# Eight edits to a scheduled one-core transformer layer: sums of the start on TensorE, decay factors by ScalarE, half-row modulation, the last gate folded into w_down

## The chip, the cores and the metric

One Trainium2 chip, one NeuronCore (core 0). The metric is the device time of one execution in microseconds (us). Engines are named as in the profile: PE is TensorE's matmul stream, PEld its weight loads, DVE is VectorE, ACT is ScalarE, POOL is GpSimd, SP is the engine that issues every DMA of this kernel (SPq its queue).

## The reference, cut to what matters

Batch 1, 512 positions, width 1024, one layer, float32.

```python
mod = (silu(c) @ ada_w + ada_b)[:, None, :]
sh1, sc1, g1, sh2, sc2, g2 = jnp.split(mod, 6, axis=-1)
h = x * (1.0 + sc1) + sh1
# mixer: proj = h @ w_in (1024 x 4112), split into q, k, v (8 heads x 64), z, xBC, dt (16 columns)
#   attention: block-sparse causal, ALiBi
#   xBC = silu(causal_dwconv(xBC, 4 taps)) -> xs (16 heads x 64), B, C (2 groups x 128)
#   dt = softplus(dt_raw + dt_bias); a = -exp(a_log)
#   y = ssd_scan(xs, dt, a, B, C) + xs * d_skip     (decays exp(cumsum(dt * a)))
#   y = grouped_rms_norm(y * silu(z)) * norm_w;  o = [attention, y] @ w_out
x = layer_norm(alpha * x + (1.0 + g1) * o, ln1_g, ln1_b)
h = x * (1.0 + sc2) + sh2
u = causal_dwconv(h @ w_up, 3 taps)                 # 1024 x 5632
y = (silu(u[:, :2816]) * u[:, 2816:]) @ w_down      # 2816 x 1024
out = layer_norm(alpha * x + (1.0 + g2) * y, ln2_g, ln2_b)
```

## The kernel before, in words

**The order of work.** The kernel doesn't write its instructions down in a fixed order. Each piece of work is a Python generator ("thread") that yields one engine operation, a buffer request or a `Need` of a key at a time. `Order.run` holds a modelled clock for each engine, asks every thread for its next operation, and emits the one with the earliest modelled start; ties within a small slack go to the lowest priority number given in `R.spawn(thread, priority)`. Durations come from `Order.price`. All operations are emitted in `Order.emit`, which is line 300, so nearly every row of the profile says L300 and groups are told apart by their tiles. What results is one fixed sequence for each engine; at run time each engine works through its own, and waits for the others by semaphores. A changed price, priority or thread can therefore move any later instruction.

**Matmuls.** A float32 matrix is split into a rounded high part (ACT copy, `wh`, `hh`) and the remainder (DVE subtract, `wl`, `hl`), and each product is three passes in TensorE's rounded format: high by high, low by high, high by low. A weight item of 128x1024 values is `raw` when it has landed; `w_load` requests it and `w_split` makes `wh` and `wl`.

**The start.** `start_load` issues for each of eight blocks k of 128 channels: four 256 KB pieces of the first two modulations' weights (`aw`), the block of x (`xk`) and 128 rows of the w_in columns of B, C and four x tiles (`wr`, 128x768). For each block `start_acc` multiplies `aw` by the activated conditioning vector and adds it up on DVE into two partial sums `acc[:, 0]` and `acc[:, 1]`, and adds these two; `start_h` sums over partitions with PE (`pa`), makes `mod`, then `hh`, `hk`, `hl`. `products` runs six accumulators (`first`) over the blocks. `start_dt` loads and splits the 16 dt columns (`wdr`); `consts` loads three 16-value vectors by broadcast and builds masks.

**The mixer.** Then come the remaining projection tiles (`fm`, and `tm` for v). `dt_chain` turns the dt product (`pd`) into time steps: transposed by `pdt` with the 0/1 matrix `sel`, some 20 small DVE operations (`dd`), cumulative sums by PE (`pcs`), copied (`csT`) and written to a scratch array in DRAM (`drcs`) by four DMAs. `ssd_decay(ft)`, for each of eight pairs of heads, reads from there twice: `er` (64 partitions x 3 x 128, twice), then one ACT exponential of 128x384; and `csb`, the whole 4 KB row on all 128 partitions, masked by POOL (`affine_select`), eight ACT exponentials, two DVE multiplies by the scores `sc`, and then the stationary operand of PE's `py`. `ssd_state` makes `xe`, `pst`, `st`, `pyo`. Attention, gate, norm, out_proj (`po` from `os`), and the first layer norm follow; meanwhile `ada_mid` sums up three more modulations, and `x_rows` reads x again.

**The end.** The up projection (`up`, convolution `u`, gated product `mid`), then w_down (`dn`) in two column halves, the second in column pieces so that the last layer norm (`ln2`) can start; there `y = dn * g2p` and `XN = XN + y` on DVE, statistics `st`, `mv`, normalisation and the output DMAs.

## Time and profile before

| | us |
|---|---|
| three timed runs | 726.88, 727.51, 728.98 (median 727.51) |
| the profiled execution, own time | 729.33 |
| its span on the page | 727.6 |
| PE busy in the span | 711.1 (98%) |
| PEld, DVE, ACT, POOL busy | 582.4, 528.1, 314.3, 58.7 |
| moved by DMA | 98.95 MB, mean 136 GB/s |

The page divides the span into 40 slices; in nearly all PE is busy for nine tenths or more. Whatever the time can lose must come from the few places where PE is idle or slow, or from fewer PE passes. "Idle before, releaser" in a row is how long an engine sat idle before that instruction and what ended it. Times at the left of a timeline row are us from the start of the span, then the us that the row covers.

### The profile page before, as it was taken

To read this page: it belongs to the slowest core of one execution; us is meant where nothing else is said; L and a number is where in the kernel's file an instruction comes from. 1 tells how busy PE (TensorE), PEld (TensorE's weight loads), DVE (VectorE), ACT (ScalarE), POOL (GpSimd) and SP (SyncE) were. 2 spreads that over 40 slices of the span, in tenths; PEclk is the share of its full clock that TensorE was granted. 3 is DMA by queue.
4 is the path that set the end of the run, shared out by engine and by line. 5 is a ranking of instruction groups with operands and counts; after the bars stand their busy time and mean duration, and the time that the engine had idled before them with its cause. 6 is when DMAs were issued, how large, how long until landed. Compare 5 with 4: busy or idle time off the path is not lost.

```text
span 727.6 us, 9568 instructions
## 1 busy us (share of the span) xinstructions
PE 711.1 (98%) x3603; PEld 582.4 (80%) x3603; DVE 528.1 (73%) x935; ACT 314.3 (43%) x524; POOL 58.7 (8%) x68
## 2 busy tenths in 40 slices
PE   8999989999999999999999999999999999999995
PEld 8776867788887888788998888888888888888885
DVE  5988899999998998597865886565665664227247
ACT  2447475564665643233753443434444452212100
POOL 0010101110000011001000000000000009300022
PEclk9999999999999999999999999999999999999999
DMA  9995677426235845243623553323333254322202
GB/s 260 308 255 169 143 215 205 125 74 198 88 96 170 280 156 177 62 133 90 174 87 116 174 155 102 91 86 95 105 90 89 69 165 160 97 87 88 86 30 86
DMA packets 115831, 98.95 MB, mean 136 GB/s; under 512 B 5325, under 2 KB 97865, under 8 KB 115785
## 3 DMA queue, kind: packets, MB, share of 16 engines
q1 hardware_dynamic: 115785, 98.34, 46.0%
q8 instruction: 28, 0.46, 0.3%
q14 instruction: 18, 0.15, 0.1%
HBM read 96.20 MB, written 2.13 MB: 135 GB/s over the span
## 4 chain that ended last, share of the span: by engine, by line
PE 57%; DVE 1%; issue 0%; DVEq 0%
PE up L300 34%; PE dn L300 17%; PE po L300 6%; PE pt L300 0%; DVE XN L300 0%; PE pad L300 0%; DVE st L300 0%; DVE y L300 0%; DVE mv L300 0%; DVEq L1602 0%
## 5 line engine op out<-in xcount | busy, mean ns | idle before, releaser
L300 DVE TENSOR_TENSOR wl<-raw,wh 128x1024 fp32r<-128x1024 f32 x102 | 127.5, 1252 | 88.1 <-ACT wh L300 77.0
L300 ACT ACTIVATE wh<-raw 128x1024 fp32r<-128x1024 f32 x102 | 106.9, 1051 | 87.5 <-PE dn L300 54.5
L300 PE MATMUL up<-h2h,wh 128*128 128x512 f32 (+1 forms) x384 | 144.4, 376 | 0.0
L300 PE MATMUL up<-h2h,wl 128*128 128x512 f32 (+1 forms) x384 | 144.3, 376 | 0.0
L300 PE MATMUL up<-h2l,wh 128*128 128x512 f32 (+1 forms) x384 | 144.0, 375 | 0.0
L300 PE MATMUL dn<-wh,mid 128*128 128x512 f32 (+1 forms) x356 | 102.7, 372 | 0.0
L300 DVE SCALAR_TENSOR_TENSOR u<-up,fprm,u 128x511 f32<-128x511 f32 x88 | 65.8, 749 | 34.9 <-ACT u L300 33.3
L300 PEld LDWEIGHTS up<-h2h,wl 128*128 128x128 f32 x384 | 72.2, 188 | 14.2
L300 PEld LDWEIGHTS up<-h2l,wh 128*128 128x128 f32 x384 | 72.2, 188 | 14.0
L300 PEld LDWEIGHTS up<-h2h,wh 128*128 128x128 f32 x384 | 72.3, 188 | 13.9
L300 PEld LDWEIGHTS dn<-wh,mid 128*128 128x128 f32 x356 | 64.7, 188 | 12.6
L300 PE MATMUL fm<-hh,wh 128*128 128x512 f32 x176 | 72.9, 414 | 1.1 <-DVE BT L300 1.1
L300 PE MATMUL fm<-hh,wl 128*128 128x512 f32 x176 | 69.4, 395 | 0.0
L300 PE MATMUL fm<-hl,wh 128*128 128x512 f32 x176 | 69.3, 394 | 0.0
L300 PE MATMUL dn<-wl,mid 128*128 128x512 f32 (+1 forms) x178 | 66.2, 372 | 0.0
L300 ACT ACTIVATE u<-up,fprm 128x512 f32<-128x512 f32 x44 | 34.2, 777 | 50.6 <-PE up L300 50.6
L300 POOL TENSOR_TENSOR XN<-XN,l 128x512 f32<-128x512 f32 x16 | 25.0, 1582 | 244.0 <-ACT l L300 243.4
L300 PE MATMUL po<-wh,os 128*128 128x512 f32 x128 | 42.4, 397 | 0.3 <-DVE os L300 0.3
L300 PEld LDWEIGHTS fm<-hh,wh 128*128 128x128 f32 x176 | 33.2, 188 | 8.3 <-ACT CT L300 1.6
L300 PEld LDWEIGHTS fm<-hh,wl 128*128 128x128 f32 x176 | 33.1, 188 | 7.8
L300 PEld LDWEIGHTS dn<-wl,mid 128*128 128x128 f32 x178 | 33.5, 188 | 6.3
L300 DVE SCALAR_TENSOR_TENSOR acc<-ad,csil,acc 128x1024 f32<-128x1024 f32 x28 | 36.5, 1304 | 2.7 <-DMA ad<-in_ada_w_dram 2.7
(226 smaller groups left out, 1057.5 us busy)
## 6 DMA issues: line engine op xcount, KB each, us to landing
raw<-in_ffn_up_w_dram SPq DMA_DIRECT2D x44, 512.0 KB, 3.9
ad<-in_ada_w_dram SPq DMA_DIRECT2D x32, 512.0 KB, 5.0
raw<-in_mix_in_w_dram SPq DMA_DIRECT2D x26, 512.0 KB, 7.0
raw<-in_ffn_down_w_dram SPq DMA_DIRECT2D x22, 512.0 KB, 3.9
aw<-in_ada_w_dram SPq DMA_DIRECT2D x32, 256.0 KB, 6.0
raw<-in_mix_out_w_dram SPq DMA_DIRECT2D x12, 512.0 KB
csb<-drcs SPq DMA_DIRECT2D x8, 512.0 KB
wr<-in_mix_in_w_dram SPq DMA_DIRECT2D x8, 384.0 KB
```

Source lines behind the costliest of these rows:

```text
L300: getattr(self.hw[op.eng], op.fn)(*op.args, **op.kw)
```

## The change

1. **Sums of the start.** In blocks 1, 3, 5, 7 the DVE addition of the two partial sums is dropped; PE's `pa` sums both (eight passes of one column instead of four). In block 0 the order of `pa`'s passes changes, and the high part of `wr` is copied by DVE instead of ACT.
2. **dt weights.** `wr` is 784 columns wide and brings them; `wdr`, its DMA and `start_dt` go. Each block splits its 16 columns (one ACT, one DVE operation of 128x16).
3. **Constants.** The three vectors come as one row and are broadcast by one PE matmul (`pc`); `sel` is made in `consts`, at priority 6.
4. **Order of the six accumulators** in `products`: 3, 5, 2, 4, 0, 1.
5. **Decays.** `csT` is made in the order of its readers and written by one DMA; `er` is no longer read from DRAM but is an ACT exponential of `csb` in two halves of 64 partitions, before POOL masks `csb`.
6. **Late modulations** are split into high and low by half rows, at items 3, 10, 16 instead of 3, 11, 19, at another priority; `x_rows` starts later.
7. **Last gate.** The second column half's w_down weights are multiplied by `g2p` on DVE when they have landed; `ln2` then adds `dn` directly there.
8. **Prices** of DMAs, ACT operations with a pointer operand and long POOL operations in the planner.

By count, PE has 3354 instructions instead of 3346, DVE 948 instead of 935, ACT 511 instead of 490, POOL 62 as before, and SP issues 230 DMAs instead of 250.

```diff
             ap = [a.ap for a in outs + ins if a.tensor.name.startswith(("in_", "out_", "dr"))][-1]
             run = 4 * (ap[-1][1] if ap[-1][0] == 1 else 1)
-            return max(size / 3.5e5, size / run * (0.008 + 3.71e-5 * run) / 16)
+            return max(size / 3.5e5, size / run * (0.007 + 4.0e-5 * run) / 16)
...
-            return 0.06 + 0.001 * n
+            return 0.06 + 0.001 * n + (0.5 if n > 512 else 0)
...
     def consts():
-        yield Need("wdr")
-        drow = yield buf("t", [P, 8, 2], "drow")
-        yield S.dma_start(dtb, row_bc(ssm_dt_bias, 0, 16))
-        yield S.dma_start(abc, row_bc(ssm_a_log, 0, 16))
-        yield S.dma_start(drow, row_bc(ssm_d, 0, 16))
+        yield Need("loads")
+        row = yield buf("s", [1, 3, 16], "row")
+        for i, src in enumerate((ssm_dt_bias, ssm_a_log, ssm_d)):
+            yield S.dma_start(row[:, i], src)
+        yield Need(("h", KC - 1))
+        pc = yield bank("mix", "pc", after=[row])
+        yield T.matmul(pc[:, :48], ones[0:1], row.rearrange("o a b -> o (a b)"), start=True, stop=True)
+        R.free(row)
+        yield V.tensor_copy(dtb, pc[:, :16])
+        yield A.activation(abc, pc[:, 16:32], AF.Exp)
+        d2 = pc[:, 32:48].rearrange("p (f h) -> p f h", h=2)
         for i in range(2):
-            yield V.tensor_copy(dcol[i * 64:(i + 1) * 64], drow[i * 64:(i + 1) * 64, :, i])
-        R.free(drow)
+            yield V.tensor_copy(dcol[i * 64:(i + 1) * 64], d2[i * 64:(i + 1) * 64, :, i])
+        R.free(pc)
+        yield V.tensor_add(sel, ident[0:32, 0:16], ident[0:32, 16:32])
         yield G.affine_select(tri, ones, pattern=[[1, P]], base=0, channel_multiplier=-1,
                               compare_op=OP.is_ge, fill=0.0)
...
-    KPE = 2
+    KPE = [2, 0, 0, 0, 0, 0, 0, 0]
+    BOTH = [0, 1, 0, 1, 0, 1, 0, 1]
...
-                wr = yield buf("b", [P, NF], "wr", "raw")
-                yield S.dma_start(wr, w_in[k * P:(k + 1) * P, 3328:4096])
+                wr = yield buf("b", [P, NF + 16], "wr", "raw")
+                yield S.dma_start(wr, w_in[k * P:(k + 1) * P, 3328:4112])
...
         R.mark("loads")
-        WR["dt"] = yield buf("s", [P, KC, 16], "wdr")
-        yield S.dma_start(WR["dt"], w_in[:, 4096:4112].rearrange("(k p) n -> p k n", p=P))
-        R.mark("wdr")
...
-            yield V.tensor_add(acc[:, 0], acc[:, 0], acc[:, 1])
+            if not BOTH[k]:
+                yield V.tensor_add(acc[:, 0], acc[:, 0], acc[:, 1])
             if n == KC:
...
-            yield A.activation(wh, wr, AF.Copy)
+            w, d = wr[:, :NF], wr[:, NF:]
+            yield A.activation(wh, w, AF.Copy) if k else V.tensor_copy(wh, w)
             WF[k] = (wh, wl)
             R.mark(("wfh", k))
-            yield V.tensor_sub(wl, wr, wh.bitcast(F32))
+            yield V.tensor_sub(wl, w, wh.bitcast(F32))
+            R.mark(("wf", k))
+            yield A.activation(wdt[:, k, 0:16], d, AF.Copy)
+            yield V.tensor_sub(wdt[:, k, 16:32], d, wdt[:, k, 0:16].bitcast(F32))
             R.free(wr)
-            R.mark(("wf", k))
-
...
-        yield V.tensor_add(sel, ident[0:32, 0:16], ident[0:32, 16:32])
         R.mark("wdt")
 
...
-                yield T.matmul(pa[:, s:s + 1], acc[:, 0, s], ones[:, 0:1], start=True, stop=not n)
                 for kc in range(KC - n, KC):
-                    yield T.matmul(pa[:, s:s + 1], AW[k][:, s, kc], csil[:, kc:kc + 1], start=False, stop=kc == KC - 1)
+                    yield T.matmul(pa[:, s:s + 1], AW[k][:, s, kc], csil[:, kc:kc + 1], start=kc == KC - n, stop=False)
+                for i in range(1 + BOTH[k]):
+                    yield T.matmul(pa[:, s:s + 1], acc[:, i, s], ones[:, 0:1], start=not n and not i, stop=i == BOTH[k])
...
@@ -694,6 +696,10 @@
         for i, (shape, _) in enumerate(items):
             yield Need(("raw", i))
             raw = RAW.pop(i)
+            if i >= len(items) - NFF // 2:
+                yield Need("g2p")
+                g2 = RES["rw"][:, 0, None, HS[1]].to_broadcast([P, 2, 512])
+                yield V.tensor_mul(raw, raw, g2)
...
-        yield A.activation(abc, abc, AF.Exp)
...
+        da2 = da.rearrange(f2)
+        dap = yield buf("d", [P, 8, NT, 2], "da")
+        yield V.tensor_copy(dap, da.rearrange("p t (f i) -> p f t i", i=2))
         pcs = yield bank("mix", "pcs")
-        da2 = da.rearrange(f2)
-        yield T.matmul(pcs[:64, 128:256], da2, tri, start=True, stop=True)
+        yield T.matmul(pcs[:64, 128:256], dap.rearrange("p f t i -> p (f t i)"), tri, start=True, stop=True)
         yield T.matmul(pcs[:, 0:64], tri, da2, start=True, stop=True)
         yield T.matmul(pcs[:, 64:128], ones, da2, start=True, stop=True)
-        R.free(da)
+        R.free(da, dap)
         csT = yield buf("s", [64, P], "csT")
         yield A.activation(csT, pcs[:64, 128:256], AF.Copy)
-        for t in range(NT):
-            yield S.dma_start(bass.AP(tensor=cs_d.tensor, offset=cs_d.offset + 2 * t * P,
-                                      ap=[[2 * NT * P, 8], [P, 2], [1, P]]), csT[16 * t:16 * (t + 1)])
+
+        yield S.dma_start(cs_d, csT)
         R.mark("csd")
         R.free(csT)
...
         yield Need("dt")
-        er = yield buf("s", [P, NT - 1, P], "er", "er")
-        for i in range(2):
-            yield S.dma_start(er[i * 64:(i + 1) * 64],
-                              bass.AP(tensor=cs_d.tensor, offset=cs_d.offset + (2 * NT * ft + 2 + i) * P,
-                                      ap=[[0, 64], [2 * P, NT - 1], [1, P]]))
         c_ = yield buf("b", [P, NT, 2, P], "csb", "csb")
         yield S.dma_start(c_.rearrange("p t h l -> p (t h l)"),
                           bass.AP(tensor=cs_d.tensor, offset=cs_d.offset + 2 * NT * ft * P,
                                   ap=[[0, P], [1, 2 * NT * P]]))
-        yield A.activation(er, er, AF.Exp)
+        er = yield buf("s", [P, NT - 1, P], "er", "er")
+        for i in range(2):
+            q = slice(i * 64, (i + 1) * 64)
+            yield A.activation(er[q], c_[q, 1:, i], AF.Exp)
...
-    def ada_sum(idx, item):
+    def ada_half(acc, n):
+
+        hl_ = yield buf("b", [P, 2, 512], "acch", dt=F32R)
+        yield A.activation(hl_[:, 0], acc[:, HS[n]], AF.Copy)
+        yield V.tensor_sub(hl_[:, 1], acc[:, HS[n]], hl_[:, 0].bitcast(F32))
+        pa = yield bank("mix", "pad", [hl_])
+        yield [T.matmul(pa, ones_r, hl_[:, i], start=i == 0, stop=i == 1) for i in range(2)]
+        R.free(hl_)
+        return pa
-        hi = yield buf("b", [P, DM], "acch", dt=F32R)
-        lo = yield buf("b", [P, DM], "accl", dt=F32R)
-        yield A.activation(hi, acc, AF.Copy)
-        yield V.tensor_sub(lo, acc, hi.bitcast(F32))
-        R.free(acc)
-        return hi, lo
...
+    ADA0, ADA1, ADA2 = 3, 10, 16
 
     def ada_mid():
         yield Need(("item", 2))
-        yield from ada_row(2, "g1p", ROWS, 3)
+        yield from ada_row(2, "g1p", ROWS, ADA0)
...
-        yield Need(("oa", 3))
+        yield Need(("oa", 3), *(("os", k) for k in range(8)))
...
             q = r[:, c0:c1]
-            y = yield buf("s", [P, c1 - c0], "y2")
-            yield V.tensor_mul(y, ps[t, c0][:, :c1 - c0], g2p[:, c0:c1])
-            R.free(ps[t, c0])
-            yield V.tensor_add(q, q, y)
-            R.free(y)
+            if c0 < 512:
+                y = yield buf("s", [P, c1 - c0], "y2")
+                yield V.tensor_mul(y, ps[t, c0][:, :c1 - c0], g2p[:, c0:c1])
+                R.free(ps[t, c0])
+                yield V.tensor_add(q, q, y)
+                R.free(y)
+            else:
+                yield V.tensor_add(q, q, ps[t, c0][:, :c1 - c0])
+                R.free(ps[t, c0])
             yield V.bn_stats(st[:, i], q)
...
-                for m in range(6):
+                for m in (3, 5, 2, 4, 0, 1):
...
-    R.spawn(start_dt(), 3)
...
-    R.spawn(ada_mid(), 8)
+    R.spawn(ada_mid(), lambda: 3 if wpos[0] > 16 else 8)
```

Three places where the planner's sequences differ. **ACT, where the first three decays are made.** `er` and `csb` are as above, `th` and `Y` belong to the convolutions, `wh` to a weight item, `qk` to attention. Before:

```order
L300 ACTIVATE er_827<-er_827 128x384
L300 ACTIVATE th_886<-Y_651 128x512
L300 ACTIVATE qk_758<-fm_691,qs_83 64x512
L300 ACTIVATE Y_651<-fm_818,prm_76 128x512
L300 ACTIVATE csb_846<-csb_846,ncs_86 128x128 x4
L300 ACTIVATE qk_758<-fm_757 64x512 x2
L300 ACTIVATE csb_846<-csb_846,ncs_86 128x128 x3
L300 ACTIVATE qk_758<-fm_757 64x512 x2
L300 ACTIVATE csb_846<-csb_846,ncs_86 128x128
L300 ACTIVATE er_828<-er_828 128x384
L300 ACTIVATE csb_857<-csb_857,ncs_86 128x128
```

With the change:

```order
L300 ACTIVATE wh_960<-raw_659 128x1024
L300 ACTIVATE er_978<-csb_955 64x384 x2
L300 ACTIVATE th_1003<-Y_652 128x512
L300 ACTIVATE er_980<-csb_956 64x384 x2
L300 ACTIVATE st_983<-pst_1014 128x128
L300 ACTIVATE wh_1016<-raw_802 128x1024
L300 ACTIVATE er_985<-csb_957 64x384 x2
L300 ACTIVATE csb_955<-csb_955,ncs_86 128x128 x8
L300 ACTIVATE csb_956<-csb_956,ncs_86 128x128 x8
L300 ACTIVATE csb_957<-csb_957,ncs_86 128x128 x8
```

Before, the exponentials of a `csb` were mixed with other work and came as each landed; now three pairs of `er` operations, each of which needs its `csb` landed, stand ahead of all 24 exponentials, with two weight copies and the copy of a state (`st`) between them.

**SP, where the cumulative sums go out and come back.** `raw` is a weight item, `ad` a piece of a late modulation. Before:

```order
L300 DMA raw_762<-in_mix_in_w_dram 128x2x512
L300 DMA drcs<-csT_798 8x2x128 x4
L300 DMA raw_823<-in_mix_in_w_dram 128x8x128
L300 DMA er_827<-drcs 64x3x128 x2
L300 DMA csb_846<-drcs 128x1024
L300 DMA er_828<-drcs 64x3x128 x2
L300 DMA csb_857<-drcs 128x1024
L300 DMA er_829<-drcs 64x3x128 x2
L300 DMA csb_876<-drcs 128x1024
L300 DMA ad_903<-in_ada_w_dram 128x1024
```

With the change:

```order
L300 DMA ad_876<-in_ada_w_dram 128x1024
L300 DMA drcs<-csT_932 64x128
L300 DMA raw_962<-in_mix_in_w_dram 128x8x128
L300 DMA csb_955<-drcs 128x1024
L300 DMA csb_956<-drcs 128x1024
L300 DMA csb_957<-drcs 128x1024
L300 DMA raw_1018<-in_mix_in_w_dram 128x8x128
```

Four writes have become one, six reads of `er` have gone, and the three `csb` stand together.

**DVE, from the last convolution of B and C to the dt chain's first operation.** Before:

```order
L300 SCALAR_TENSOR_TENSOR CT_649<-first_104,prm_76,CT_649 128x509
L300 SCALAR_TENSOR_TENSOR BT_648<-first_101,prm_76,BT_648 128x511
L300 SCALAR_TENSOR_TENSOR BT_648<-first_101,prm_76,BT_648 128x510
L300 SCALAR_TENSOR_TENSOR CT_649<-th_670,CT_649 128x512
L300 TENSOR_TENSOR dd_711<-pdt_690,dtb_80 128x64
L300 TENSOR_SCALAR dd_712<-dd_711 128x64
L300 TENSOR_TENSOR dd_712<-dd_712,dd_711 128x64
```

With the change:

```order
L300 SCALAR_TENSOR_TENSOR Y_652<-th_771,Y_652 128x512
L300 SCALAR_TENSOR_TENSOR Y_652<-first_100,prm_76,Y_652 128x509
L300 TENSOR_TENSOR wl_731<-raw_624,wh_730 128x1024
L300 SCALAR_TENSOR_TENSOR Y_652<-th_789,Y_652 128x512
L300 COPY dcol_82<-pc_618 64x8 x2
L300 TENSOR_TENSOR wl_801<-raw_635,wh_800 128x1024
L300 TENSOR_TENSOR sel_78<-ident_68 32x16
L300 SCALAR_TENSOR_TENSOR qk_839<-fm_696,qs_83,qk_839 64x512 x2
L300 TENSOR_TENSOR dd_849<-pdt_838,dtb_80 128x64
L300 TENSOR_SCALAR dd_850<-dd_849 128x64
```

Before, the dt chain's first `dd` followed a convolution of C. Now it stands 23 rows later, behind the convolutions of both C groups and two x tiles, and `sel`, which `pdt` needs, has moved there from the start.

## Rows read from the trace of the kernel before

**Rows 1.** The page, busy time of PE.

```profile
PE 711.1 (98%) x3603; PEld 582.4 (80%) x3603; DVE 528.1 (73%) x935; ACT 314.3 (43%) x524; POOL 58.7 (8%) x68
```

**Rows 2.** Windows: stretch, length, busy us per engine, granted clock, DMA share, GB/s.

```profile
4.00:48.00 44.00, 41.83 (x209) 34.19 (x208) 36.40 (x95) 16.33 (x22) 0.00 (x0) 0.96 1.12 303
...
302.00:719.70 417.70, 417.40 (x1974) 345.83 (x1973) 255.59 (x341) 153.54 (x200) 36.11 (x29) 1.00 0.35 105
719.70:727.60 7.90, 0.00 (x0) 0.00 (x0) 4.57 (x11) 0.00 (x0) 1.42 (x2) 0.82 0.30 106
...
11.30:14.70 3.40, 3.40 (x16) 3.30 (x16) 3.01 (x9) 1.45 (x2) 0.00 (x0) 0.50 1.14 317
...
100.04:103.46 3.42, 3.30 (x13) 2.59 (x14) 3.10 (x5) 3.42 (x8) 0.00 (x0) 0.50 0.19 34
```

**Rows 3.** Waits of PE: total us, times, longest us.

```profile
PE py L300 <- DVE csb L300: 2.0, 1, 2.0
PE first L300 <- POOL half L300: 1.4, 1, 1.4
```

**Rows 4.** Timeline of PE around the end of the wait for `csb`.

```profile
96.52 0.40 PE L300 MATMUL tm<-wh,hl 128*128 128x512 f32 x1
96.75 0.40 PE L300 MATMUL tm<-wh,hh 128*128 128x512 f32 x1
...
100.16 1.12 PE L300 MATMUL py<-csb,xd 128*64 128x128 f32 x8 [1.96 <-DVE csb L300]
```

**Rows 5.** Timeline of the end, DVE.

```profile
719.73 0.42 DVE L300 TENSOR_TENSOR y<-dn,RW 128x256 f32<-128x256 f32 x1 [0.18 <-PE dn L300]
720.19 0.42 DVE L300 TENSOR_TENSOR XN<-XN,y 128x256 f32<-128x256 f32 x1
```

**Rows 6.** Timeline of the last start block, DVE and PE.

```profile
51.27 0.42 DVE L300 TENSOR_TENSOR acc<-acc 128x256 f32<-128x256 f32 x1
...
52.38 0.50 PE L300 MATMUL pa<-ones_r,acc 128*128 128x1 f32 x4
```

**Rows 7.** Timeline of PE, the first projection tile after the start.

```profile
63.24 0.47 PE L300 MATMUL fm<-hh,wh 128*128 128x512 f32 x1 [1.13 <-DVE BT L300]
```

**Rows 8.** Groups of DVE: a convolution's step, and the weights' low part.

```profile
L300 DVE SCALAR_TENSOR_TENSOR BT<-first,prm,BT 128x511 f32<-128x511 f32 x2 | 1.5, 744 | 0.2 <-ACT BT L300 0.2
...
L300 DVE TENSOR_TENSOR wl<-raw,wh 128x1024 fp32r<-128x1024 f32 x102 | 127.5, 1252 | 88.1 <-ACT wh L300 77.0 <-issue 8.2 <-PE dn L300 2.6
```

**Rows 9.** Timelines of SP and POOL: `csb` issued, and masked when landed.

```profile
81.80 0.53 SPq L300 DMA_DIRECT2D csb<-drcs  x1
...
87.61 1.10 POOL L300 TENSOR_SCALAR_AFFINE_SELECT csb<-csb 128x1024 f32<-128x1024 f32 x1 [34.33 <-DMA csb<-drcs]
...
85.62 0.54 SPq L300 DMA_DIRECT2D csb<-drcs  x1
...
92.56 1.10 POOL L300 TENSOR_SCALAR_AFFINE_SELECT csb<-csb 128x1024 f32<-128x1024 f32 x1 [1.00 <-DMA csb<-drcs]
...
148.18 0.55 SPq L300 DMA_DIRECT2D csb<-drcs  x1
...
152.44 1.10 POOL L300 TENSOR_SCALAR_AFFINE_SELECT csb<-csb 128x1024 f32<-128x1024 f32 x1 [9.30 <-DMA csb<-drcs]
```

**Rows 10.** Timeline of SP: `csT` written, and the first read of it.

```profile
76.26 2.81 SPq L300 DMA_DIRECT2D drcs<-csT  x4
...
80.37 1.33 SPq L300 DMA_DIRECT2D er<-drcs  x2
```

**Rows 11.** Groups of ACT and DVE on the decays and states.

```profile
L300 ACT ACTIVATE er<-er 128x384 f32<-128x384 f32 x8 | 4.1, 517 | 3.7 <-DMA er<-drcs 3.7
...
L300 ACT ACTIVATE csb<-csb,ncs 128x128 f32<-128x128 f32 x64 | 20.1, 390 | 9.3 <-POOL csb L300 9.3
...
L300 ACT ACTIVATE st<-pst 128x128 f32<-128x128 f32 x8 | 2.2, 272 | 7.3 <-PE pst L300 7.3
...
L300 DVE TENSOR_TENSOR csb<-csb,sc 128x512 f32<-128x512 f32 x16 | 10.6, 685 | 0.9 <-ACT csb L300 0.8
```

More of the change, by code (lines that the diff above doesn't have):

```diff
@@ L211, in price @@
             run = 4 * (ap[-1][1] if ap[-1][0] == 1 else 1)
-            return max(size / 3.5e5, size / run * (0.008 + 3.71e-5 * run) / 16)
+            return max(size / 3.5e5, size / run * (0.007 + 4.0e-5 * run) / 16)
         ptr = sum(1 for a in ins if _n(a) == 1)
         if eng == "A":
-            return 0.04 + 0.00093 * n + (0.04 + 0.07 * ptr if ptr else 0) + (0.09 if "accum_out" in kw else 0)
+            return 0.04 + 0.00093 * n + (0.06 + 0.07 * ptr if ptr else 0) + (0.09 if "accum_out" in kw else 0)
         if eng == "V":
@@ L576, in start_acc @@
             acc = yield buf("s", [P, 2, 2, P], "acc")
-            n = KC - KPE if k == 0 else KC
+            n = KC - KPE[k]
             for kc in range(n):
@@ L597, in start_w @@
             wl = yield buf("b", [P, NF], "wlf", "wl", F32R)
-            yield A.activation(wh, wr, AF.Copy)
+            w, d = wr[:, :NF], wr[:, NF:]
+            yield A.activation(wh, w, AF.Copy) if k else V.tensor_copy(wh, w)
             WF[k] = (wh, wl)
             R.mark(("wfh", k))
-            yield V.tensor_sub(wl, wr, wh.bitcast(F32))
+            yield V.tensor_sub(wl, w, wh.bitcast(F32))
+            R.mark(("wf", k))
+            yield A.activation(wdt[:, k, 0:16], d, AF.Copy)
+            yield V.tensor_sub(wdt[:, k, 16:32], d, wdt[:, k, 0:16].bitcast(F32))
             R.free(wr)
-            R.mark(("wf", k))
-    def start_dt():
-        yield Need("wdr")
-        wdr = WR.pop("dt")
-        yield A.activation(wdt[:, :, 0:16], wdr, AF.Copy)
-        yield V.tensor_sub(wdt[:, :, 16:32], wdr, wdt[:, :, 0:16].bitcast(F32))
-        R.free(wdr)
-        yield V.tensor_add(sel, ident[0:32, 0:16], ident[0:32, 16:32])
         R.mark("wdt")
@@ L627, in start_h @@
             yield Need(("acc", k), ("aw", k, 4), "ada_b")
-            acc, n = ACC[k], 0 if k else KPE
+            acc, n = ACC[k], KPE[k]
             pa = yield bank("mix", "pa")
             for s in range(2):
-                yield T.matmul(pa[:, s:s + 1], acc[:, 0, s], ones[:, 0:1], start=True, stop=not n)
                 for kc in range(KC - n, KC):
-                    yield T.matmul(pa[:, s:s + 1], AW[k][:, s, kc], csil[:, kc:kc + 1], start=False, stop=kc == KC - 1)
+                    yield T.matmul(pa[:, s:s + 1], AW[k][:, s, kc], csil[:, kc:kc + 1], start=kc == KC - n, stop=False)
+                for i in range(1 + BOTH[k]):
+                    yield T.matmul(pa[:, s:s + 1], acc[:, i, s], ones[:, 0:1], start=not n and not i, stop=i == BOTH[k])
             if n:
@@ L1008, in ada_acc @@
         return acc
-    def ada_sum(idx, item):
-        acc = yield from ada_acc(idx, item)
-        hi = yield buf("b", [P, DM], "acch", dt=F32R)
-        lo = yield buf("b", [P, DM], "accl", dt=F32R)
-        yield A.activation(hi, acc, AF.Copy)
-        yield V.tensor_sub(lo, acc, hi.bitcast(F32))
-        R.free(acc)
-        return hi, lo
-    def ada_half(hi, lo, n):
-        pa = yield bank("mix", "pad", [lo])
-        yield [T.matmul(pa, ones_r, hi[:, HS[n]], start=True, stop=False),
-               T.matmul(pa, ones_r, lo[:, HS[n]], start=False, stop=True)]
+    def ada_half(acc, n):
[5 more added lines that the diff above has]
+        R.free(hl_)
         return pa
     def ada_row(idx, key, res, item):
-        hi, lo = yield from ada_sum(idx, item)
+        acc = yield from ada_acc(idx, item)
         row = yield buf("b", [P, DM], "row")
@@ L1031, in ada_row @@
         for n in range(2):
-            pa = yield from ada_half(hi, lo, n)
+            pa = yield from ada_half(acc, n)
             yield V.scalar_tensor_tensor(row[:, HS[n]], pa, 1.0, row[:, HS[n]], op0=OP.add, op1=OP.add)
             R.free(pa)
-        R.free(hi, lo)
+        R.free(acc)
         res[key] = row
@@ L1039, in ada_cols @@
     def ada_cols():
-        for idx, item in ((4, 11), (3, 19)):
-            hi, lo = yield from ada_sum(idx, item)
+        for idx, item in ((4, ADA1), (3, ADA2)):
+            acc = yield from ada_acc(idx, item)
             col = yield buf("t", [P, 8], "col")
@@ L1045, in ada_cols @@
             for n in range(2):
-                pa = yield from ada_half(hi, lo, n)
+                pa = yield from ada_half(acc, n)
                 for i in range(4):
@@ L1050, in ada_cols @@
                 R.free(pa)
-            R.free(hi, lo, junk)
+            R.free(acc, junk)
             ab = adab[:, idx * 8:idx * 8 + 8]
```

## Prediction

> **What bounds the kernel now.** I read the busy times first: PE works 711.1 us of the 727.6 us span, 98% [rows 1]. A change that leaves PE's passes as they are can gain only where PE stands still or runs slow, so I next cut the span into windows [rows 2]. The reader should see that the long stretch from 302 us to 719.7 us has 0.3 us of PE idle in 417.7, so nothing there is worth anything unless it creates a wait. The end, 7.9 us after the last matmul, has no PE at all. Then come two stretches of 3.41 us in which the granted clock is 0.50, that is 1.2 GHz instead of 2.4 GHz. The first, from 11.3 us, lies in the start, where DMA runs at a share of 1.12 and 303 GB/s and sets the pace. The second, from 100.04 us, does not. The list of PE's waits [rows 3] names what precedes it: the longest wait, 2.0 us of `py` for `csb` as DVE has multiplied it. The timeline [rows 4] places that wait just before 100.16 us. Waits of 1.4 us [rows 3] and 1.13 us [rows 7] also exist; the 1.13 us one was followed by no fall of the clock. Everything else is shorter.
>
> So there are three sources of time: the wait for `csb` (1.96 us), the half clock behind it (3.41 us at half rate do the work of 1.71 us, so 1.71 us are lost), and the 7.9 us end. Together with what the start may lose, the change is judged on these.
>
> **The end (part 7).** The chain there is `y`, then `XN`, then statistics, each waiting for the one before. `y` starts at 719.73 and `XN` at 720.19 [rows 5]. For the last column piece `y` goes, so 0.46 us go. In exchange DVE multiplies 11 weight items by `g2p`. Each is a 128x1024 operation on two operands, as `wl` is, 1252 ns [rows 8]: 13.8 us of DVE, and in `ln2` 3 products of 512 columns fewer and 2 of 256. DVE is busy 255.6 of 417.7 us in that stretch [rows 2], so it has room, and the multiplies come before their copy and subtraction, which are made several items ahead. I take -0.46 us; if that cover failed, each item would delay PE by at most its 1.25 us, which stays in the range only for one or two items.
>
> **The decays (part 5).** Before, `csb` 0 was issued at 81.80 us and masked at 87.61; the third was issued at 85.62 and masked at 92.56 [rows 9], each behind two reads of `er`. The reads go. So do three of four writes of `drcs`: from the last of them, issued some 0.6 us before 79.1, to the first read at 80.37 [rows 10] passes about 1.9 us, which is the write's latency and stays.
>
> But the planner now starts the whole dt chain later, and this has to be walked. PE's first projection tile starts at 63.24 [rows 7]. Up to `pdt` the changed order has 63 passes of 512 columns, start to start 0.23 us (96.52 to 96.75 [rows 4]), 14.6 us, and 14 float32 products of 128 columns, about 0.22 us each by the same rows scaled (two passes), 3.1 us: `pdt` is reached at 80.9 us. On DVE, `BT`'s three steps start three times 0.744 us [rows 8] before the tile, at 60.8 us. Up to `sel` come 24 convolution steps and gates, 17.9 us, two `wl`, 2.5 us, and small ones, less the few tenths by which neighbours overlap: 81.3 us. So `pdt` waits about 0.45 us for `sel`, a new wait. Bounds: 0 and 1.5 us, the latter if nothing on DVE overlaps.
>
> From there the 20 small DVE operations take as long as before, `csT` is copied at about 90.3 us instead of 76, written at 90.6, read from 92.5, with the three `csb` 0.6 us apart. To landing, the rows give 4.26 us for one issued in a quiet stretch (148.18 to 152.44) and 5.8 to 6.9 us for three behind each other [rows 9]. The quiet value lands the three at 96.8, 98.5 and 100.3, since 512 KB take 1.7 us at 303 GB/s; the crowded value lands them at 98.3, 100 and 101.8. On ACT the halves of `er` cost as much as the whole, 517 ns [rows 11], since its width is the same: 16 of them instead of 8, 4.1 us more on an engine that is busy 43% [rows 1]. Then come 24 exponentials and two 685 ns multiplies per `csb` [rows 11].
>
> PE meets its first need of this at `pyo`, about 102.3 us. That needs the state, whose copy (272 ns [rows 11]) stands on ACT behind the second pair of `er`: ready at 101.1 to 102.6 us. `py` 0 comes at about 108.4 us, after 93 full passes (21.5 us) and 17 small products from `pdt`'s end at 82.4 us. Its `csb` has been exponentiated by about 105.5 and multiplied by 107; the next two are ready some 0.8 and 1 us ahead of their `py`. Before, PE wanted the second `csb` at 98.2 us and had it at 100.16 [rows 4]; now it wants it at about 109.1 and has it at 108.3: PE comes 10.9 us later, `csb` 8.1 us. What closes the gap is that the three `csb` are now issued together, 1.2 us from first to last instead of 3.8 us. The wait of 1.96 us goes, and the half clock, 1.71 us, with it. The bound on the other side is that all of it comes back.
>
> **The start (parts 1 to 4).** The addition that goes took 0.42 us in the last block, between the last piece of weights and `pa`; `pa`'s four passes took 0.50 us [rows 6], and eight will take 1.0 us. Net +0.08 us in the odd blocks, on the path only in the last, which is odd. Where PE rather than DMA sets a block's pace, the whole 0.5 us counts: up to 2.0 us over four blocks. The 16 extra columns per row make 64 KB in eight blocks, 0.2 us at 303 GB/s. I take +0.2 us, with bounds -0.4 us (only the addition counts) and +2.2 us. The 1.13 us wait before the first projection tile is ended by `BT` and not by weights, so the earlier request for weights behind it gains nothing. That the clock falls in a block with eight one-column passes is not excluded either: it did fall at 11.3 us [rows 2].
>
> **The rest (parts 6 and 8).** The late modulations move the same work in smaller pieces. The other waits are below 1 us each, in places that the planner fills again; I keep them and give them bounds of -1 and +1.5 us.
>
> **The sum.** -0.46 - 1.96 - 1.71 + 0.45 + 0.2 = -3.5 us. Against the profiled execution, 729.33 us (span 727.6), that is 725.8 us; this execution lay 1.8 us above the median, so against the median of 727.51 us the forecast is **724.0 us**. A measurement of this kernel tells about 0.3% from no change, 2.2 us: below 725.3 is faster, above 729.7 slower.
>
> **The rivals.**
>
> *A: the wait moves.* The dt chain is 14 us later, with new needs (`sel`, `pyo`, three `csb` in a row) whose margins are 0 to 1.5 us by my walk. If one of them waits 2 us and the clock halves again behind it, -3.67 us is lost from the sum: 727.7 us, no change. For it: margins this thin come from sums of dozens of durations. Against it: each is positive with the quiet landing, and a wait under 1.2 us brought no half clock.
>
> *B: slower, by the head of ACT's queue.* ACT's rows show each operation starting only after the one listed before it, and the changed order puts three pairs of `er`, which need landed `csb`, ahead of the state's copy, two weight copies and all exponentials. If the second `csb` lands later than 100.3 us, `pyo` waits; from about 102.3 us on, 2 us later, the wait reaches the length that halved the clock, and `py` waits again for exponentials that began as much later. Two such pairs cost 2 x 3.67 us, where one was taken out: 731.3 us. For it: 6.9 us from issue to mask has been seen [rows 9], and a weight item is issued just ahead. Against it: the reads of `er` no longer share the engines. The Trainium skill's Perfetto Trace Analysis (Tensor Engine Instruction) says that ACT, DVE and GpSimd execute strictly first in, first out, which is this rival's mechanism; the rows of ACT agree so far as they go. The skill's DMA: Bandwidth & Descriptors (Anatomy of one DMA) gives about 2.0 us plus bytes at 436 GB/s, an estimate of 3.2 us for 512 KB; the trace's 4.3 to 6.9 us disagree, and by the page's figure every margin would be a microsecond wider and this rival nearly out.
>
> *C: the start grows.* If the odd blocks are set by PE, +2.2 us replaces +0.2 us: 726.0 us, no change by the bound; with one half clock in the start, 727.7 us.
>
> **How the numbers follow.** The forecast has 0.57, of which I count 0.07 as gains too small to tell; A 0.17; C 0.12, a third of it still below 725.3; B 0.14. Faster: 0.50 + 0.04 = 0.54. Same: 0.07 + 0.17 + 0.08 = 0.32. Slower: 0.14. The range goes from 721.5 us (start -0.4, no wait for `sel`, other waits -1, rounded down) to 728.5 us, which takes in A and C with some of the other waits; B lies outside, and little of the low side.
>
> **What would show it.** Right: no PE wait for `csb`; granted clock 1.00 from 15 us to the last matmul; the end 7.4 us instead of 7.9; `pdt` waits some tenths for `sel`; the first projection tile at 63.2 to 63.6 us. A shows as one wait near 2 us between 80 and 130 us with half clock behind it; B as two, at `pyo` and `py`, ended by ACT or DVE, with `er` idle on a DMA; C as a first projection tile after 64.5 us. The forecast is wrong if the span from 130 us on is not the same within a microsecond apart from the end, since nothing in the sum comes from there.

## The result, and the profile after

| | before | changed |
|---|---|---|
| timed runs, median (lowest to highest) | 727.73 us (726.88 to 728.98), 6 runs | 723.97 us (723.17 to 725.04), 6 runs |
| profiled execution | 729.33 us, span 727.6 | 723.32 us, span 721.6 |

The ratio is 0.9948 with a 95% interval of 0.9935 to 0.9961: 3.8 us faster. The forecast was 724.0 us. The two profiled spans differ by 6.0 us, more than the medians: the profiled execution of before lay 1.6 us above its median, that of the changed kernel 0.65 us below. A comparison of the two traces alone therefore overstates the change, and a part of this document is to find out by what.

The windows of the changed kernel, with the columns of [rows 2]:

```profile
4.00:48.00 44.00, 41.45 (x223) 34.20 (x223) 37.23 (x103) 17.10 (x30) 0.00 (x0) 1.00 1.08 304
...
98.00:104.00 6.00, 5.74 (x27) 4.33 (x26) 4.38 (x8) 5.90 (x17) 3.11 (x2) 1.00 0.74 214
...
302.00:713.90 411.90, 411.90 (x1951) 341.05 (x1951) 265.81 (x351) 151.48 (x199) 36.49 (x29) 1.00 0.35 108
713.90:721.60 7.70, 0.31 (x3) 0.10 (x1) 4.14 (x10) 0.00 (x0) 0.99 (x1) 0.73 0.28 99
```

Both stretches of half clock of [rows 2] are absent, and the long stretch is again without idle. PE's waits in the changed kernel, against [rows 3]:

```profile
PE first L300 <- ACT hh L300: 1.7, 4, 0.8
PE fm L300 <- DVE mx L300: 1.4, 1, 1.4
PE first L300 <- POOL half L300: 1.4, 1, 1.4
PE ps L300 <- DMA prow<-in_ada_b_dram: 0.5, 1, 0.5
PE py L300 <- issue: 0.5, 1, 0.5
PE px L300 <- DVE mod L300: 0.3, 1, 0.3
PE pyo L300 <- ACT st L300: 0.2, 1, 0.2
```

The 2.0 us of `py` for `csb` [rows 3] are gone. A new wait of 1.4 us for `mx` (a small tile of attention, at 205 us) has come. On ACT the first two pairs of `er` each wait for their `csb` and the state's copy stands behind them, as the order showed; `pyo` waits 0.24 us for it. (What the copy reads, `pst`, was done on PE at 96.27 us; the copy came 2 us later, right behind the second pair.)

```profile
95.10 1.07 ACT L300 ACTIVATE er<-csb 64x384 f32<-64x384 f32 x2 [3.57 <-DMA csb<-drcs]
...
97.16 1.07 ACT L300 ACTIVATE er<-csb 64x384 f32<-64x384 f32 x2 [0.33 <-DMA csb<-drcs]
98.25 0.28 ACT L300 ACTIVATE st<-pst 128x128 f32<-128x128 f32 x1
...
100.60 7.14 ACT L300 ACTIVATE csb<-csb,ncs 128x128 f32<-128x128 f32 x24
```

```profile
98.58 1.38 PE L300 MATMUL pyo<-CT,st 128*128 128x128 f32 x6 [0.24 <-ACT st L300]
...
105.46 1.97 PE L300 MATMUL py<-csb,xd 128*64 128x128 f32 x32
```

The end, against [rows 5], one step shorter:

```profile
714.24 0.42 DVE L300 TENSOR_TENSOR XN<-XN,dn 128x256 f32<-128x256 f32 x1 [0.59 <-PE dn L300]
714.70 0.43 DVE L300 BATCH_NORM_STATS2 st<-XN 128x6 f32<-128x256 f32 x1
```

The last matmul ends at 714.21 us and 7.37 us follow, where 7.93 followed before.

### The profile page after: what moved, and what is told of

Read it like the earlier page. It is cut to its first block, busy times and chain, and to the rows that moved or that the text cites. A ratio compares the mean times of both kernels' runs of the same rounds, so it can differ in the third digit from the quotient of the medians.

```text
span 721.6 us, 9608 instructions
## 1 busy us (share of the span) xinstructions
PE 708.0 (98%) x3619; PEld 581.2 (81%) x3619; DVE 535.6 (74%) x948; ACT 320.0 (44%) x545; POOL 57.5 (8%) x68
## 4 chain that ended last, share of the span: by engine, by line
PE 88%; DMA 4%; SPq 4%; DVE 3%; issue 1%; ACT 1%; DVEq 0%; ACTq 0%
PE up L300 34%; PE dn L300 17%; PE fm L300 15%; PE po L300 9%; SPq L300 4%; PE tm L300 2%; DMA aw<-in_ada_w_dram 2%; PE pov L300 1%; PE first L300 1%; PE psS L300 1%; PE py L300 1%; PE pT L300 1%; DVE acc L300 1%; DMA csb<-drcs 1%; DMA ad<-in_ada_w_dram 1%
```

## The experiments

All twelve stand in one table, worked out from their profiles. "First tile" is the start of the first projection tile [rows 7]. "Mixer" is from there to the first `up` matmul. "Waits" are PE's waits over 0.2 us in it, the first tile's own left out, added up; "half" is the time at half clock in it. "Left" is the mixer less the waits less half of what PE was busy at half clock. "Rest" is from the first `up` to the end of the span.

| kernel | first tile | mixer | waits | half | left | rest | profiled | timed median (runs) |
|---|---|---|---|---|---|---|---|---|
| before | 63.24 | 286.24 | 3.42 | 3.41 | 281.2 | 378.1 | 729.33 | 727.73 (6) |
| e1 before again | 64.21 | 284.49 | 3.18 | 0 | 281.3 | 378.1 | 728.55 | 728.16 (10) |
| e2 before + start | 61.84 | 287.07 | 5.29 | 3.41 | 280.1 | 378.0 | 728.60 | 729.60 (10) |
| e3 before + decays | 63.40 | 286.30 | 3.70 | 3.41 | 280.9 | 377.4 | 728.77 | 729.00 (10) |
| e4 before + gate | 61.89 | 287.99 | 5.34 | 3.41 | 280.9 | 377.7 | 729.35 | 727.83 (10) |
| e10 before + prices | 62.78 | 285.64 | 4.46 | 0 | 281.2 | 378.7 | 728.80 | 728.91 (10) |
| changed | 61.36 | 282.47 | 2.17 | 0 | 280.3 | 377.8 | 723.32 | 723.97 (6) |
| e9 changed again | 62.15 | 282.62 | 2.00 | 0 | 280.6 | 377.8 | 724.26 | 725.22 (5) |
| e12 changed, old order of accumulators | 62.04 | 282.14 | 1.88 | 0 | 280.3 | 377.7 | 723.66 | 724.22 (4) |
| e6 changed, one sum | 62.73 | 284.24 | 2.61 | 0 | 281.6 | 377.5 | 726.16 | 724.91 (10) |
| e5 changed, old transfers | 72.42 | 281.83 | 1.79 | 0 | 280.0 | 377.9 | 733.87 | 733.35 (4) |
| e7 changed, er by DMA | 65.31 | 288.23 | 5.55 | 0 | 282.7 | 377.4 | 732.68 | 732.77 (4) |
| e8 changed, old prices | 63.89 | 295.29 | 8.24 | 13.65 | 282.3 | 377.8 | 738.67 | 738.73 (4) |
| e11 changed, old late modulation | 64.11 | 304.31 | 21.3 | 20.48 | | 378.7 | 748.87 | 749.51 (4) |

"Left" stays between 280.0 and 282.7 us and "rest" between 377.4 and 378.7; most of what differs is the start, the waits, and the half clock. But 2.7 us of "left" are not small beside a gain of 3.8, and no run tells what they consist of: between the executions of one order named below it differs by at most 0.4 us. (For e11 the waits include 2.4 us of the first `up` itself, and "left" is not formed: its half clock fell mostly into the wait for `acch`.)

Six of these profiles belong to two orders alone. In e1 every engine's sequence is that of before, in e4 up to the first `up`; in e9 every engine's sequence is that of the changed kernel, and e12 differs from it only in which accumulator comes first in `products`. So the mixer of before took 284.5 to 288.0 us in three executions (mean 286.2), that of the changed kernel 282.1 to 282.6 (mean 282.4).

**e1, the kernel before once more.** The kernel is unchanged.

> The kernel before, unchanged, profiled once more. Its first profile was 729.33 us, 1.6 us above its median of 727.73; that of the changed kernel 0.65 us below its median. Theory: the two waits that went (1.96 us for csb, then 3.41 us at half clock) belong to every execution: both show again at 98 to 104 us, and the execution is within 1 us of 729.3. Rival: the half clock behind that wait, or that at 11.3 us, comes only in some executions; then the profile shows it missing and the execution is 1.5 to 1.8 us shorter. Timed ratio 1.000 within 0.002 either way.

Ratio 1.0014 (1.0001 to 1.0027). Although the kernel is the same, the interval leaves out 1.000; differences of one or two tenths of a per cent are therefore not read in what follows. The `csb` wait was there again, 2.25 us, but no half clock behind it; instead the start had 10.24 us of it:

```profile
101.32 0.66 PE L300 MATMUL py<-csb,xd 128*64 128x128 f32 x8 [2.25 <-DVE csb L300]
```

```profile
101.20:104.70 3.50, 3.38 (x27) 2.55 (x28) 3.19 (x5) 3.50 (x8) 0.00 (x0) 1.00 0.35 85
8.44:18.68 10.24, 10.21 (x42) 9.68 (x43) 7.07 (x17) 4.18 (x6) 0.00 (x0) 0.50 1.14 318
```

So the rival is right on the clock: the 1.71 us that I had put on that stretch belong to some executions only. (e4 has it there again, from 99.68 to 103.10 us.)

What it is worth in the mean can be read from the timed runs, since each has its mean granted clock on record. Of 58 executions of the kernel before, timed beside e1 to e12, 20 had a clock of 0.996 or more and took 727.36 us in the mean; 18 had 0.992 or less and took 727.73 us. For scale, one stretch of 3.41 us at half clock lowers the mean clock by 0.002. So executions with hardly any half clock before the end were only 0.4 us shorter, and still some 3 us longer than the changed kernel. Where in the run the clock fell is not on record for them.

**e2 to e4, parts alone on the kernel before.**

```diff
e2: parts 1 to 4 of the change, nothing else
e3: part 5, nothing else
e4: part 7, nothing else
```

> The kernel before with the start's edits alone (sums by PE in odd blocks, dt weights along w_in, constants by one row, order of the accumulators). Theory: the first projection tile starts at 61.2 to 61.6 us instead of 63.24, without the 1.13 us wait for BT; PE's work after it is the same, so 725.3 to 726.3 us unless the new order makes its own wait. Rival (the start's gain is lost again, as what follows was waiting for DMA or DVE anyway): the tile at 61.4 but the first up matmul no earlier than 349 us, and 727 to 728 us.

> The kernel before with the decays' edit alone (er by ACT from csb, csT by one DMA). Theory: the reads of er were what kept csb late; with them gone the wait of 1.96 us before py goes, and the half clock behind it: 723.8 to 725.0 us. Rival: what closed the gap in the changed kernel is that the whole dt chain came 12 us later, after more matmuls; then with the early dt chain py still waits 1 to 3 us, for er at the head of ACT's queue, and the time is 726.5 to 729 us.

> The kernel before with the last gate's edit alone. Theory: the end after the last matmul shrinks from 7.9 to 7.4 us and nothing else moves before w_down: 727.2 to 727.4 us, which timing can't tell from no change; no wait of PE in w_down. Rival: the multiply delays a weight item, seen as a PE wait for wh or wl in w_down of 0.3 us or more, and the gain is lost.

Ratios: e2 1.0031 (1.0011 to 1.0052), e3 1.0030 (1.0013 to 1.0048), e4 1.0005 (0.9993 to 1.0017). Neither the start nor the decays gain anything alone. Both read 0.3% slower, which is little more than the 0.14% of the unchanged kernel in e1. PE's waits in e2 and in e3:

```profile
PE py L300 <- ACT wh L300: 3.0, 1, 3.0
PE py L300 <- issue: 1.8, 1, 1.8
```

```profile
PE pn L300 <- DVE z L300: 1.5, 1, 1.5
...
PE py L300 <- DVE csb L300: 0.8, 1, 0.8
...
PE po L300 <- DVE os L300: 0.5, 1, 0.5
```

In e2 the first tile came at 61.84 us, near the 61.2 to 61.6 expected (though e4, with the start of before, had it at 61.89), and `py` waited 4.9 us instead of 2, with 3.41 us of half clock behind the second of these waits: whatever the start had gained was given back. The time, 729.60 us, fits neither theory. In e3 the `csb` wait fell to 0.8 us, as the theory had it, but `pn` waited 1.5 us for the gate at 255 us with 3.41 us of half clock behind, where nothing waited before: the planner had placed the later work anew. The time is the rival's, its reason is not. In e4 the end shrank from 7.93 to 7.46 us with no wait in w_down, as the theory had it; too little for the timing to show. In its mixer, where no row of any engine had moved, a second `py` waited 2.5 us, which neither before nor e1 shows: so waits of this size also come and go between executions of one order.

**e5, the dropped transfers put back for nothing.**

```diff
+        wd = yield buf("s", [P, KC, 16], "wdr")
+        yield S.dma_start(wd, w_in[:, 4096:4112].rearrange("(k p) n -> p k n", p=P))
+        bd = yield buf("t", [P, 8, 2], "drow")
+        for v in (ssm_dt_bias, ssm_a_log, ssm_d):
+            yield S.dma_start(bd, row_bc(v, 0, 16))
+        R.free(wd, bd)
         R.mark("loads")
```

> The changed kernel with the four transfers that it dropped put back for nothing (1024 rows of 64 B and three broadcasts of 16 values, issued on SP just ahead of the small parameter loads and the weights), everything else in the same order but for a few passes of the last start block. Theory: in the kernel before, the 1.13 us wait of the first projection tile was at bottom a late landing of the third weight item, which stood ahead of BT at the head of ACT's queue; so the same transfers here delay the weight requests by 1 to 2 us, ACT idles on raw by 0.5 to 2 us, BT is late and the first tile starts at 62 to 63.2 us instead of 61.36; 724.6 to 725.8 us. Rival: the wait went because of the new order of the accumulators, which completes BT's first; then the first tile starts within 0.3 us of 61.4 and the time is 723.5 to 724.5 us.

The time was 733.35 us, a ratio of 1.0070 (1.0046 to 1.0093), and the first tile came at 72.42 us, which neither theory had. My three broadcasts wrote the same tile and so waited for one another, and the small parameter loads behind them came 3.2 us late for PE. The clock fell during this wait and stayed at half for 13.65 us:

```profile
54.94 0.36 PE L300 MATMUL ps<-ident,prow 76*128 76x76 f32 x1 [3.16 <-DMA prow<-in_ln_b_dram]
```

```profile
53.85:67.50 13.65, 12.56 (x34) 9.91 (x35) 5.63 (x8) 5.46 (x7) 3.52 (x14) 0.50 0.98 310
```

It shows how costly a delay on SP is there, and decides nothing between the two theories. Other profiles do that better. With the rows of the start as in before, ACT's third weight copy waited for its landing 1.59 us in the first profile of before, 2.28 in e3, 0.67 in e4 and not at all in e1; PE's first tile then waited 1.13, 1.68, and in e4 and e1 less than 0.2 us:

```profile
58.28 1.06 ACT L300 ACTIVATE wh<-raw 128x1024 fp32r<-128x1024 f32 x1 [1.59 <-DMA raw<-in_mix_in_w_dram]
```

```profile
56.93 1.06 ACT L300 ACTIVATE wh<-raw 128x1024 fp32r<-128x1024 f32 x1 [0.67 <-DMA raw<-in_mix_in_w_dram]
```

(The first is the kernel before, the second e4.) The wait that the trace put down to `BT` was a late weight at the head of ACT's queue, with the convolution behind it. It can come with the start of the changed kernel as well: in e11, whose rows are the changed kernel's up to 190 us, the third and the fourth copy waited 0.71 and 0.70 us, and the first tile 0.93 us for `BT`:

```profile
59.42 1.06 ACT L300 ACTIVATE wh<-raw 128x1024 fp32r<-128x1024 f32 x1 [0.70 <-DMA raw<-in_mix_in_w_dram]
```

```profile
64.11 0.47 PE L300 MATMUL fm<-hh,wh 128*128 128x512 f32 x1 [0.93 <-DVE BT L300]
```

**e6, one sum instead of two, and e12, the old order of the accumulators.**

```diff
e6
-    BOTH = [0, 1, 0, 1, 0, 1, 0, 1]
+    BOTH = [0] * 8
e12
-                for m in (3, 5, 2, 4, 0, 1):
+                for m in range(6):
```

> The changed kernel with the DVE addition back in all eight blocks and four passes of pa in each; ACT's and SP's order unchanged. Theory: a block is set by DMA, so only the last block shows the difference, 0.42 us of addition against 0.5 us of passes: mod of block 7 within 0.4 us of 51.6 us, time within 0.6 us of 724.0. Rival: DVE sets the blocks' pace (its work per block is about as long as the transfers), the additions add 0.4 us in four blocks: mod of block 7 at 52.6 to 53.3 us and 725.0 to 725.7 us.

> The changed kernel with the six accumulators in their old order; no other row of any engine moves. Theory: BT's first convolution waits for the third and fourth weight item at the head of ACT's queue, not for its accumulator, so the order is worth under 0.4 us: first projection tile at 61.3 to 61.8 us, 723.5 to 724.6 us. Rival: BT's accumulator is completed up to 1.15 us later (five passes of 0.23 us) and the wait for BT comes back: first tile at 62.3 to 62.6 us, 724.7 to 725.2 us.

e6 took 724.91 us, 0.9960 (0.9947 to 0.9974) of before, 0.9 us above the changed kernel's first median and below its second (e9), so there is no difference that these runs can tell. `mod` of block 7 came at 52.96 us instead of 51.59, but from block 1 to block 6 both took 28.9 to 29.1 us (17.38 to 46.43 and 17.15 to 46.02): the additions of blocks 3 and 5, 0.42 us each, lengthen it by 0.2 us in all, so DVE does not set the pace there. DMA, at a share of 1.08 in the window from 4 to 48 us, fits. Most of the rest, 1.0 us, is the last block, where a small parameter load was 0.5 us late in this execution and `pa` stood behind more passes of `first`. e12 took 724.22 us, and its first tile came at 62.04 us with 3.41 us of half clock in the start and no wait for `BT`: the order is worth nothing that shows.

**e7, e8, e11: a part taken out of the changed kernel.**

```diff
e7: part 5 undone      e8: part 8 undone      e11: part 6 undone
```

> The changed kernel with er read from DRAM again and csT written by four DMAs. Theory: the reads of er delay each csb and the chain is as late as in the changed kernel, so py waits for csb 2 to 4 us, sometimes with half clock: 726.0 to 729.5 us. Rival (it was the later place of the dt chain, after more matmuls, that closed the gap): py waits less than 0.7 us in all and the time is 723.5 to 725.0 us.

> The changed kernel with the planner's old prices, nothing else. With them the planner puts the dt chain early again (pdt is PE's row 202 instead of 260). Theory: where the waits fall is the planner's doing; with the early chain py comes before csb again and PE waits 2 to 5 us for it in all: 726 to 729.5 us. Rival: the edits themselves carry the gain wherever the chain stands: 723.5 to 725.0 us, csb waits under 0.7 us.

> The changed kernel with the late modulations as before (split as 128x1024, at items 3, 11, 19, priority 8, x read early). Theory: that part matters only through where DVE's wait for its weights falls: the wait of 1.45 us for mx at 205 us behind a late piece of modulation changes place, others come; mixer waits of 2 to 6 us in all, 724 to 728 us. Rival: the part is worth nothing either way, mixer waits within 0.7 us of 2.2 and 723.5 to 724.6 us.

Ratios to before: e7 1.0070 (1.0054 to 1.0086), e8 1.0161 (1.0134 to 1.0188), e11 1.0277 (1.0249 to 1.0305). Each lacks one part and is slower than before. But not for the reason that I had given: in e7, with `er` read from DRAM, no `py` waited over 0.2 us; `pT` waited for the gate before out_proj instead. (Of the 9.4 us by which its profile is longer than the changed kernel's, 4.0 lie ahead of the first tile, where its rows are the changed kernel's and 10.24 us ran at half clock; 3.4 are waits in the mixer and 2.4 "left", and the rest is 0.3 shorter.) In e8 the chain stood early again and `py` waited only 0.8 us for `csb`; the time went at the end of the mixer. The wait of e7, that of e8 and its window of half clock, and that of e11:

```profile
PE pT L300 <- DVE z L300: 2.8, 1, 2.8
```

```profile
PE pr L300 <- DVE mx L300: 4.4, 1, 4.4
```

```profile
272.81:286.46 13.65, 9.56 (x24) 6.80 (x25) 12.13 (x38) 4.31 (x10) 1.02 (x1) 0.50 0.00 0
```

```profile
PE pad L300 <- ACT acch L300: 18.0, 1, 18.0
```

In e11 the third late modulation isn't summed up when out_proj is done. DVE waits for its last pieces, which SP issued only at 344.59 and 348.54 us, between weight items of the up projection; ACT waits for DVE, PE for ACT, and the up projection, which needs the sum, starts 25 us later (368.4 instead of 343.8 us):

```profile
351.46 1.28 DVE L300 SCALAR_TENSOR_TENSOR acc<-ad,csil,acc 128x1024 f32<-128x1024 f32 x1 [1.81 <-DMA ad<-in_ada_w_dram]
356.28 1.28 DVE L300 SCALAR_TENSOR_TENSOR acc<-ad,csil,acc 128x1024 f32<-128x1024 f32 x1 [3.54 <-DMA ad<-in_ada_w_dram]
```

That it misses by so much was in neither theory; both had this part at 0 to 4 us.

**e9 and e10: the changed kernel once more, and the prices alone.**

> The changed kernel, unchanged, profiled once more. Theory: its time is the start up to the first projection tile (61.36 us in its first profile), about 280.3 us of PE work to the first up matmul plus the waits and half clock in it (2.2 us there), and 377.8 us for the rest; the start is the part that differs between executions. So: mixer stretch within 1 us of 282.5 us, up to the end within 0.5 us of 377.8, and the first tile between 61 and 63 us unless the clock halves in the start; timed median 723.5 to 724.6 us. Rival: the waits in the mixer differ as much between executions as between kernels; then the mixer stretch differs by over 2 us from 282.5.

> The kernel before with the planner's new prices alone. Theory: prices decide where PE waits, and only together with the edits do they give the good order: here the dt chain stays early (pdt is PE's row 199) and csb is still read behind er, so py waits 2 us or more and 726 to 730 us. Rival: the new prices are the better model as such and carry the gain: the csb wait under 0.7 us and 723.5 to 725.5 us.

e9 took 725.22 us, 0.9953 (0.9933 to 0.9972); the mixer was 282.62 against 282.47 us and the rest the same, as the theory had it; only its median lies 0.6 us above what I had expected. For the order of before the rival would have been right: its mixer differed by 3.5 us between e1 and e4. In e9, too, the 1.4 us wait for `mx` had become 0.8 us at another instruction. e10 took 728.91 us, 1.0012 (0.9998 to 1.0027). Here no `py` waited over 0.2 us, although `er` is still read from DRAM; but `psS`, `pT`, `pxt`, `po` and `pr` waited 0.7 to 1.2 us each, 4.5 us with the first tile's own left out. The theory's time is right, its reason is not.

None of the variants is faster than the changed kernel by more than its own two medians, 723.97 and 725.22 us, lie apart.

## Why the prediction was right, and where only its number was

**The end: right.** Forecast -0.46 us; the end went from 7.93 to 7.37 us, and from 7.93 to 7.46 in e4, with no new wait in w_down.

**The wait for `csb`: right for this kernel, wrong as the price of part 5.** Forecast -1.96 us, and it went; `pyo` waited 0.24 and 0.45 us in the two profiles of the changed kernel, where my walk (101.1 to 102.6 us against 102.3) allowed at most 0.3; it stood some 3.7 us earlier on the clock, as everything did. From the end of `pdt` to `py` 0 passed 25.8 us against the 26.0 that I had stated, though the terms that I had named for it add up to 25.2. But e3 got most of it by part 5 alone, e10 all of it by prices alone, and e7 kept it gone without part 5. It is a property of the finished order, and a walk of that order, not a price of the part, is what the number rested on. The landing came out between the ends of the rows: the three `csb` were issued from 89.98 us on,

```profile
89.98 1.30 SPq L300 DMA_DIRECT2D csb<-drcs  x3
```

and the first pair of `er` began at 95.10 us, 5.1 us later, where 4.3 and 5.8 us had bounded it. The 3.2 us estimated from the Trainium skill's DMA: Bandwidth & Descriptors (Anatomy of one DMA) were too short again; the page gives that fit for transfers issued by GpSimd, and these are issued by SP. The measurement decides. That ACT works strictly in order, which the Trainium skill's Perfetto Trace Analysis (Tensor Engine Instruction) says, the rows of ACT bear out: the state's copy began 2 us after its input was ready, right behind the second pair of `er`.

**The half clock: mis-sized.** Forecast -1.71 us, as if it came in every execution. In the profiles of before and e4 it stood behind the wait, in e1 it did not, after a longer wait. Over the timed executions of before, those with hardly any half clock were only 0.4 us shorter than those with the most. So the term took one profile for every execution. In the mean it is worth less than 1.71 us: 1.1 by the three profiles of that order, nearer to 0.4 by the timed runs.

**`sel`: wrong.** Forecast +0.45 us. `sel` was made at 77.85 us and `pdt` ran at 78.63, without a wait. From the first tile on, my walk of DVE's rows was 1.6 us too long (81.3 less 63.24 against 77.85 less 61.36 us), and that of PE's rows 0.4 us; the lower bound was the right end.

**The start: the term held only as a mean, and one step in it was wrong.** Forecast +0.2 us; the two profiles show -1.9 us. That is between executions: four profiles with before's rows in the start (before, e1, e3, e4) have the first tile at 61.9 to 64.2 us, four with the changed kernel's (changed, e7, e9, e11) at 61.4 to 65.3 us, and the mean of both is 63.2 us. From block 1 to block 7 `mod` takes 34.60 us before and 34.44 after, so the sums are indeed worth nothing there. The step that was wrong is "ended by `BT` and not by weights, so the earlier request for weights behind it gains nothing": `BT` was itself behind a weight copy on ACT that waited for DMA. In the two profiles of the changed kernel the last such wait is 0.2 to 0.3 us and the first tile doesn't wait; in e11, with the same rows, it waits 0.93 us. So the releaser was misread, but that the earlier request gains something is not shown: these profiles show no gain, and e5, which was to settle it, overshot.

**The other waits: inside the bounds.** I kept them. Those of before (`xe` 0.55, `oa` 0.63, `os` 0.29 us) went, `mx` 1.45 and `py` 0.49 us came: +0.5 us. Beyond that "left" fell by some 0.7 us, which I had not forecast and cannot explain; the mixer has the same PE passes in both kernels, in another order. From the first `up` to the last matmul 370.2 us became 370.4, so nothing of the gain comes from there, as forecast. Between 130 us and the first `up` the order itself differs, and that part of the sign can't be read exactly.

**The sum.** Between the two profiles: start -1.9, mixer -3.8, rest -0.4 (the end -0.56, the stretch before it +0.17), 6.0 us in all. The second pair, e1 and e9, gives -2.1, -1.9 and -0.4, 4.3 us. Over all profiles of either order the start gives nothing, the mixer -3.8 (286.2 to 282.4: about -2.0 by waits, -1.1 by half clock, -0.7 by "left") and the rest -0.4 us. The forecast of -3.5 us against a measured -3.8 us came out of errors of opposite sign: the half clock counted in full made the gain too large, the wait for `sel` that didn't come and the fall of "left" that I had not seen made it too small. That the wait for `csb` goes had been walked; that the sum came so close is partly luck.

**The rivals.** A came in part: a stall of 1.45 us, but without half clock. B did not come, although its place was right: the margin at `pyo` was used up, by 0.24 and 0.45 us of waiting. C did not come in the two profiles of the changed kernel. A first tile after 64.5 us did show in e7, with the same rows there and 10.24 us of half clock; but e1, with before's rows and as much half clock, has it at 64.2. e5 shows that a late small load can make the start 10 us longer.

## What to carry to other kernels

Where a planner fixes the order, parts of a change have no prices of their own: four pieces (the start, the decays, the last gate, the prices), each alone on the kernel before, gained nothing that shows, and each of three parts taken out of the changed kernel made it 9 to 26 us slower. Walk the finished order of the whole change at the few places where an engine waits, and expect the saved time to reappear as another wait unless the walk shows otherwise. Follow a wait one step further than its releaser: if the releaser's engine was itself idle just before, the cause is what that engine waited for. And profile the kernel before more than once before a stall or a late start is counted as certain.

## What the runs showed of the hardware

The clock does not fall behind every wait of a given length. Waits in the mixer of 1.45 us (changed kernel), 2.25 us (e1), 2.54 us (e4), 2.80 us (e7) and 3.05 us (e2) were followed by the full clock, waits of 1.46 us (e3), 1.81 us (e2), 1.93 us (e4) and 1.96 us (before) by 3.41 us of half clock, at once or up to 1.5 us after PE had begun again. In the start it fell in some executions of the same order and not in others, for 3.41, 6.83 or 10.24 us, and block 1 then took 6.2 to 8.5 us instead of 5.4 to 6.0. Its longest spells (13.65 us in e5 and e8, 20.48 us in e11) began during the longest waits, of 3.2, 4.4 and 18.0 us.
